# Gate and u of an FFN tile by seven products of half-size blocks in place of eight, in a two-layer hybrid inference step

## The chip, the core and the metric

The kernel runs on one core of a Trainium2 chip. The metric is the time of one execution in device microseconds. An execution is one inference step of the whole network, and each time given below is the median of several executions or that of the one execution that the profiler recorded.

## What is computed

The network has two layers of width 1024 and works on 640 tokens, 128 of context and 512 latent ones. Layer 0 mixes tokens with a gated delta rule, layer 1 with a long convolution ("hyena"). Behind each mixer stand an out-projection and a feed-forward block (FFN), and this is the part that the change touches. Cut from the reference:

```python
def _rms_norm(x, g):
    xf = x.astype(jnp.float32)
    y = xf * lax.rsqrt(jnp.mean(xf * xf, axis=-1, keepdims=True) + EPS)
    return (y * g.astype(jnp.float32)).astype(x.dtype)

def _swiglu(h, w_gu, w_down):
    gu = h @ w_gu
    return (jax.nn.silu(gu[..., :D_FF]) * gu[..., D_FF:]) @ w_down
...
        ctx = ctx + mc[2] * oc
        lat = lat + ml[2] * ol
        ctx = ctx + mc[5] * _swiglu(_modulate(_rms_norm(ctx, norm2_g[layer]), mc[3], mc[4]),
                                    ffn_w_gu[layer], ffn_w_down[layer])
        lat = lat + ml[5] * _swiglu(_modulate(_rms_norm(lat, norm2_g[layer]), ml[3], ml[4]),
                                    ffn_w_gu[layer], ffn_w_down[layer])
```

`w_gu` is 1024 x 5632: its first 2816 columns make the gate, the other 2816 make u. `_modulate(h, shift, scale)` is `h * (1 + scale) + shift` with other vectors for context and latent tokens.

## The kernel before

Activations lie transposed: features on the 128 partitions, tokens along the free axis, so that a tensor of width 1024 is eight tiles of 128 x 640. TensorE (PE) multiplies in a reduced-precision 32-bit type, fp32r. So each operand is held as a high part, its cast to that type, and a low part, the rest; and one product is three matmuls, high x high, high x low and low x high, added in one PSUM bank. ScalarE (ACT) makes high parts by a cast, VectorE (DVE) makes low parts by a subtraction: for weights that is `wsplit`, lines 118 (`wh`) and 119 (`wl`), behind the load of a tile `raw` on SyncE's (SP) queue in `wload`. There are two buffers each of `wh` and `wl` and five of `raw`.

`out_gemm` makes the out-projection: eight rows `d`, each two halves of 24 matmuls into `ps_o`, which line 352 takes out of PSUM into the residual `x`. From each row `sumsq` (lines 247 and 248) adds up squares for the norm in `acc`, and `fold` (lines 303 to 308) makes the FFN's input as high and low parts `fh` and `fl` of 642 columns: two columns that carry the shift of context and latent tokens, then 640 tokens with the scale multiplied in. The factor of the norm itself is applied behind the products.

`ffn` walks over 22 column tiles `f` of 128 gate and 128 u columns, in three groups of 8, 8 and 6 tiles. A tile has two halves of the tokens, 322 and 320 columns wide, and in each half the gate product `ps_g` and the u product `ps_u`: 4 x 24 = 96 matmuls. Then VectorE multiplies both with the norm's factor `rbc` (lines 401 and 402), ScalarE takes Silu (line 404), VectorE multiplies gate and u (line 405), and lines 407 and 408 split the result into `hh` and `hl`. The shift arrives through the first two columns of the products, which lines 397 and 398 copy into `fb`. Behind a group stand eight down rows, `ps_d`, of 2 x 24 matmuls (2 x 18 in the third group), which line 416 adds to `x`. In the first tile the norm's factor is made: `rstd_columns` sums `acc` over partitions in `ps_ss`, `rsqrt` (lines 168 to 175) takes the inverse root on VectorE in small steps, and `rstd_rows` builds `diag` (line 270), spreads it by PE into `ps_rb` (line 276) and copies that to `rbc` (line 277).

During the third group the function `done(d)` is called behind each down row: in layer 0 it stores the row and makes the fold for the hyena mixer, in layer 1 it scales the row with the last norm's weight and transposes it for the output.

PSUM has a pool `pg` of three banks (tag "g") and in these regions a pool `pu` of five (tag "u"). A list scheduler of the framework sets the order on each engine from the written order and the dependencies, ahead of the run; an engine then runs its list in order. Each tag of a pool is a ring of buffers, and who takes a buffer waits until its last readers are done.

Of the kernel before, what the change touches and what calls it, by code (L numbers as in the profile page):

```python
# [25 lines left out]
KD = D // 128  # L26
# [4 lines left out]
RAWS = 5  # L31

# [55 lines left out]
class _Kernel:  # L88
# [153 lines left out]
    def sumsq(self, pool, acc, x, first):  # L242
        if first:
            self.A.activation(acc, x, AF.Square)
        else:
            sq = pool.tile([128, NTOK], F32, tag="sq", name="sq", bufs=1)
            self.A.activation(sq, x, AF.Square)
            self.V.tensor_add(acc, acc, sq)
# [62 lines left out]

    def split_x(self, k, src):
# [16 lines left out]
    def out_gemm(self, pool, pu, src, xs, gate, x_old, ab, bias=None):  # L329

        V = self.V
        fx = []
        acc = pool.tile([128, NTOK], F32, tag="acc", name="acc", bufs=1)
        x = []
        for d in range(KD):
            xo = pool.tile([128, NTOK], F32, tag="xo", name="xo", bufs=2)
            self.nc.sync.dma_start(xo, x_old[d])
            w = self.wtile(src, 0, KD, d * 128)
            xt = pool.tile([128, NTOK], F32, tag=f"x{d}", name=f"x{d}", bufs=1)
            for hf in range(2):  # L340
                psp, tag = (self.pg, "g") if (2 * d + hf) % 8 < 3 else (pu, "u")
                ps = psp.tile([128, 512], F32, tag=tag, name="ps_o")
                self.gemm(ps[:, :320], w, xs, HALVES[hf])
                for c, sl, pl in PIECES[hf]:
                    g = gate[:, c, d : d + 1]
                    if bias is not None:
                        ob = pool.tile([128, 320], F32, tag="ob", name="ob", bufs=2)
                        self.A.activation(ob[:, pl], ps[:, pl], AF.Identity, bias=bias[:, d : d + 1])
                        src_ = ob[:, pl]
                    else:  # L350
                        src_ = ps[:, pl]
                    V.scalar_tensor_tensor(out=xt[:, sl], in0=src_, scalar=g, in1=xo[:, sl],
                                           op0=ALU.mult, op1=ALU.add)
# [7 lines left out]
    def ffn(self, pool, pg, pu, layer, x, acc, xs, done):  # L361
# [3 lines left out]
        gate = self.mod[layer][:, :, 40:48]  # L365

        for f0, nf, slots in ((0, 8, range(8)), (8, 8, (8, 9, 10, 11, 0, 1, 2, 3)),
                              (16, 6, (12, 13, 8, 9, 10, 11))):
            hs = []
            for f in range(f0, f0 + nf):  # L370
                wg = self.wtile(I["ffn_w_gu"][layer], 0, KD, f * 128)
                wu = self.wtile(I["ffn_w_gu"][layer], 0, KD, DFF + f * 128)
# [6 lines left out]
                prods = []
                for hf in range(2):  # L380
                    fs = (slice(0, 322), slice(322, 642))[hf]
                    o = 2 - 2 * hf
                    p1 = pg.tile([128, 512], F32, tag="g", name="ps_g")
                    self.gemm(p1[:, : 320 + o], wg, xs, fs)
                    p2 = pu.tile([128, 512], F32, tag="u", name="ps_u")
                    self.gemm(p2[:, : 320 + o], wu, xs, fs)
                    prods.append((p1, p2))
                    if hf == 0 and rb is None:
                        rs = self.rstd_columns(pool, pu, "u", acc)
# [1299 lines left out]
```

## Time and profile before

| | |
|---|---|
| median of three runs | 2105.75 us (2103.25 to 2108.15) |
| the profiled execution, its own time | 2103.4 us |
| span of that execution in the trace | 2101.6 us |
| granted clock of TensorE, mean over the span | 0.989 |
| matmuls in the trace | 13779 |
| DMA | 237.01 MB, 113 GB/s in the mean |

A page of the profile lists the busy time of each engine, its share of the span, the chain of work that ended last, and groups of instructions by line, with busy time, mean duration of one in ns, idle time in front of them and who ended it. PEld is the loading of weights into TensorE, which runs beside the matmuls. The trace is the same execution instruction by instruction, with start times in us from the start of the span.

### The profile page before, as it was taken

The numbers are of one execution on the slowest core, as the hardware profiler recorded it, in microseconds if no ns is written. First come the engines' busy times: TensorE is split into PE (matmuls) and PEld (weight loads), VectorE is DVE, ScalarE is ACT, GpSimd is POOL, SyncE is SP. The second block draws the span as 40 slices with busy tenths as digits, with TensorE's granted clock in tenths as the row PEclk, the third lists the DMA queues.
The fourth block names the chain that finished last, engine by engine and source line by source line (L and its number), as shares of the span: only waits on it lengthen the run. The fifth ranks groups of instructions, "written<-read, shape, count | busy, mean of one in ns | idle before, by whom it ended". The sixth has DMA issues, their size and how long they took to land.

```text
span 2101.6 us, 34710 instructions
## 1 busy us (share of the span) xinstructions
PE 2033.6 (97%) x13779; PEld 1889.1 (90%) x13779; DVE 1260.7 (60%) x2649; ACT 794.1 (38%) x1761; POOL 135.6 (6%) x241
## 2 busy tenths in 40 slices
PE   7998999999989999999999999999999999999997
PEld 4677888988866899999999999999889999999997
DVE  6887887876654464434434467878775443443444
ACT  4456445555533443212222243333344321221222
POOL 0131011110110100000000001010000000000000
PEclk8999999999989999999999999999999999999998
DMA  7856453344555632222222253222453222222221
GB/s 236 274 184 154 113 153 100 83 124 115 183 180 181 200 119 62 79 81 70 72 81 71 58 162 100 82 85 76 141 161 95 72 81 71 71 81 71 71 63 58
DMA packets 344833, 237.01 MB, mean 113 GB/s; under 512 B 62274, under 2 KB 314810, under 8 KB 344671
## 3 DMA queue, kind: packets, MB, share of 16 engines
q1 hardware_dynamic: 322495, 230.18, 36.7%
q10 hardware_dynamic: 22176, 4.62, 1.1%
q8 instruction: 108, 1.77, 0.4%
q14 instruction: 54, 0.44, 0.1%
HBM read 202.57 MB, written 32.19 MB: 112 GB/s over the span
## 4 chain that ended last, share of the span: by engine, by line
PE 81%; DVE 7%; ACT 4%; DMA 3%; issue 2%; POOL 0%; ACTq 0%; POOLq 0%; DVEq 0%
PE ps_g L131 15%; PE ps_u L131 15%; PE ps_d L131 15%; PE ps_hp L143 8%; PE ps_o L131 5%; PE ps_p L143 4%; PE ps_ada L209 2%; PE ps_ab L1467 2%; PE ps_g L1524 2%; PE ps_gate L143 1%; PE ps_s L1248 1%; PE ps_s L1214 1%; PE ps_y L1161 1%; PE ps_s L1225 1%; DMA ft<-fa 1%
## 5 line engine op out<-in xcount | busy, mean ns | idle before, releaser
L118 ACT CAST wh<-raw 128x1024 fp32r<-128x1024 f32 (+2 forms) x241 | 220.8, 921 | 461.3 <-PE ps_d L131 199.3
L119 DVE TENSOR_TENSOR wl<-raw,wh 128x1024 fp32r<-128x1024 f32 (+2 forms) x241 | 257.2, 1071 | 79.1 <-ACT wh L118 78.1
L131 PE MATMUL ps_g<-fh,wh 128*128 128x320 f32 (+1 forms) x704 | 220.2, 313 | 0.0
L131 PE MATMUL ps_g<-fh,wl 128*128 128x320 f32 (+1 forms) x704 | 219.6, 312 | 0.0
L131 PE MATMUL ps_u<-fh,wh 128*128 128x320 f32 (+1 forms) x704 | 219.5, 312 | 0.0
L131 PE MATMUL ps_u<-fh,wl 128*128 128x320 f32 (+1 forms) x704 | 219.4, 312 | 0.0
L131 PE MATMUL ps_g<-fl,wh 128*128 128x320 f32 (+1 forms) x704 | 218.0, 310 | 0.0
L131 PE MATMUL ps_u<-fl,wh 128*128 128x320 f32 (+1 forms) x704 | 217.9, 310 | 0.0
L416 DVE SCALAR_TENSOR_TENSOR x<-ps_d,mod,x 128x128 f32<-128x128 f32 x144 | 58.8, 437 | 154.0 <-PE ps_d L131 153.9
L131 PEld LDWEIGHTS ps_g<-fl,wh 128*128 128x128 f32 x704 | 133.6, 190 | 0.4 <-DVE fl L308 0.2
L131 PEld LDWEIGHTS ps_g<-fh,wh 128*128 128x128 f32 x704 | 133.5, 190 | 0.3 <-ACT fh L307 0.2
L131 PEld LDWEIGHTS ps_u<-fh,wh 128*128 128x128 f32 x704 | 133.6, 190 | 0.0
L131 PEld LDWEIGHTS ps_u<-fl,wh 128*128 128x128 f32 x704 | 133.4, 190 | 0.0
L131 PEld LDWEIGHTS ps_u<-fh,wl 128*128 128x128 f32 x704 | 132.8, 189 | 0.0
L131 PEld LDWEIGHTS ps_g<-fh,wl 128*128 128x128 f32 x704 | 132.5, 188 | 0.0
L143 PE MATMUL ps_p<-xh,wh 128*128 128x320 f32 x384 | 128.4, 334 | 1.8 <-ACT junk L1000 0.9
L143 PE MATMUL ps_hp<-xh,wh 128*128 128x322 f32 (+1 forms) x384 | 123.0, 321 | 0.7 <-DVE xp L1415 0.7
L143 PE MATMUL ps_p<-xh,wl 128*128 128x320 f32 x384 | 122.5, 319 | 0.0
L143 PE MATMUL ps_p<-xl,wh 128*128 128x320 f32 x384 | 122.2, 318 | 0.0
L143 PE MATMUL ps_hp<-xh,wl 128*128 128x320 f32 (+1 forms) x384 | 119.5, 311 | 0.0
L143 PE MATMUL ps_hp<-xl,wh 128*128 128x320 f32 (+1 forms) x384 | 119.4, 311 | 0.0
L131 PE MATMUL ps_d<-xh,wl 128*128 128x320 f32 x384 | 118.8, 309 | 0.0
(376 smaller groups left out, 5110.7 us busy)
## 6 DMA issues: line engine op xcount, KB each, us to landing
raw<-in_ada_w_dram SPq DMA_DIRECT2D x96, 512.0 KB
raw<-in_ffn_w_gu_dram SPq DMA_DIRECT2D x88, 512.0 KB
raw<-in_gdn_w_in_dram SPq DMA_DIRECT2D x33, 512.0 KB
raw<-in_ffn_w_down_dram SPq DMA_DIRECT2D x32, 512.0 KB
raw<-in_hy_w_in_dram SPq DMA_DIRECT2D x24, 512.0 KB
h_lat<-hlo SPq DMA_DIRECT2D x16, 512.0 KB
hs<-h_lat SPq DMA_DIRECT2D x32, 256.0 KB
raw<-in_ffn_w_down_dram SPq DMA_DIRECT2D x16, 384.0 KB
```

The lines of the kernel that those rows point to most:

```text
L118: self.A.copy(wh[:, ks, :], v[:, ks])
L119: self.V.tensor_sub(wl[:, ks, :], v[:, ks], wh[:, ks, :])
L131: self.PE.matmul(ps, a[:, k, :], b[:, sl], start=(n == 0), stop=(n == 3 * nk - 1))
L143: self.PE.matmul(ps, a[:, k, :], b[:, sl], start=(n == 0), stop=(n == 3 * nk - 1))
L209: PE.matmul(ps[32 * j : 32 * j + 32, :], self.sc[:, k, :], loaded[j * 512 // n][:, c : c + 512], start=(k == 0), stop=(k == KD - 1), skip_ ...
L416: V.scalar_tensor_tensor(out=x[d][:, sl], in0=p1[:, pl], scalar=gate[:, c, d : d + 1], in1=x[d][:, sl], op0=ALU.mult, op1=ALU.add)
L1161: PE.matmul(ps[:, n : n + 128], tm[:, d, t, :], cur[:, d, t, :], start=True, stop=True)
L1214: PE.matmul(pss[d][:, 0:128], qk[:, t, c * 128 : c * 128 + 128], state[seq, d], start=True, stop=True)
L1225: PE.matmul(p2, lt[:, d, t, c, :], ys[d], start=True, stop=True)
L1248: PE.matmul(pss[d][:, 256:384], ktok[:, t, c, :], ws[d], start=True, stop=True)
L1467: PE.matmul(ps, a_[:, m, it, js], b_[it], start=(c == 0), stop=(c == 5))
L1524: PE.matmul(pv[:, gi * 256 : gi * 256 + 256], a_[:, e, cs], b_[:, m, jt, :], start=(c == 0), stop=(c == 11))
```

## The change

The gate and u products of a tile are one product of blocks: the weights are split into two halves along the 1024 input features and into gate and u, the activations into the same two halves of features and into two halves of the tokens (322 columns each, both now with the two shift columns). Two by two blocks by two by two blocks take eight block products of 4 feature tiles x 3 matmuls; Winograd's form of Strassen's scheme takes seven, of sums of blocks, 84 matmuls in all.

- `quarters` replaces `fold` in `out_gemm`: from rows `k` and `k + 4` it makes the seven sums of activation blocks and splits each into a high part `qh` and a low part `ql`, 322 wide. The rows come in the order 0, 4, 1, 5, 2, 6, 3, 7.
- `gu_weights` makes the weights of a tile, one tile ahead of its products: it splits g in two halves, makes four sums `ws` of blocks on VectorE and splits those and one block of u into `ph` and `pl` (five buffers each).
- `gu_products` runs the seven products. Product 0's bank is copied by ScalarE into the bank in which product 2 goes on; that bank is copied after product 2 into the bank in which product 5 goes on; products 3, 4 and 6 go on in the bank of product 0 and twice in that of product 2. The matmuls that go on have no start flag.
- In `ffn` ScalarE copies product 1 to `t`, and VectorE adds `t` to two of the banks. The u results carry the opposite sign, which a negated gate of the down rows takes back. Four matmuls `ps_0` at the start of the FFN write the banks that are continued.
- The weights of the next group's first tile are made at down row 6 of a group, in front of row 7's own weights. In layer 0 `done(d)` for d of 3 and more is called behind the last down row, and the third group's `hh`, `hl` lie in other buffers.

The core of the diff:

```diff
+    def quarters(self, pool, k, hf, x, a, b, part, q):
+        A, V = self.A, self.V
+        kk = k + 4 * hf
+        f = pool.tile([128, 2, 322], F32, tag="s", name="fx", bufs=SUMS)
+        A.copy(f[:, :, 0:2], _bc(b[:, :, kk], 1, 2))
+        A.activation(f[:, 0, 2:130], x[:, 0:128], AF.Copy, scale=a[:, 0, kk : kk + 1])
+        A.activation(f[:, 0, 130:322], x[:, 128:320], AF.Copy, scale=a[:, 1, kk : kk + 1])
+        A.activation(f[:, 1, 2:322], x[:, 320:640], AF.Copy, scale=a[:, 1, kk : kk + 1])
+        B = part.setdefault(k, {})
+        B[2 * hf], B[2 * hf + 1] = f[:, 0], f[:, 1]
+        def out(i, src):
+            h, l = q[i, k] = [pool.tile([128, 322], F32R, tag=f"q{c}{i}{k}", name=f"q{c}") for c in "hl"]
+            A.copy(h, src)
+            V.tensor_sub(l, src, h)
+        tmp = lambda c: pool.tile([128, 512], F32, tag=c, name="ft", bufs=PARTS)[:, :322]
...
-        for d in range(KD):
-            xo = pool.tile([128, NTOK], F32, tag="xo", name="xo", bufs=2)
+        for n, d in enumerate((0, 4, 1, 5, 2, 6, 3, 7)):
...
-            fx.append(self.fold(*fs, d, xt, *ab))
+            self.quarters(pool, d % 4, d // 4, xt, *ab, part, fx)
...
+    def gu_weights(self, pool, layer, f, res):
+        A, V = self.A, self.V
+        W = self.I["ffn_w_gu"][layer]
+        g = self.wload(W, 0, KD, f * 128)
+        u = self.wload(W, 0, KD, DFF + f * 128)
+        def plus(x, y):
+            s = pool.tile([128, 2, 322], F32, tag="s", name="ws", bufs=SUMS)
+            s = s.rearrange("p a b -> p (a b)")[:, :512].rearrange("p (k f) -> p k f", k=4)
+            V.tensor_add(s, x, y)
+            return s
+        def out(i, src):
+            h, l = [pool.tile([128, 4, 128], F32R, tag=t, name=t, bufs=PARTS) for t in ("ph", "pl")]
+            A.copy(h, src)
+            V.tensor_sub(l, src, h)
+            res[i] = h, l
+        h, l = self.wsplit(g, 2)
+        res[0], res[3] = (h[:, 0:4], l[:, 0:4]), (h[:, 4:8], l[:, 4:8])
+        yield
+        s1 = plus(u[:, 0:4], u[:, 4:8])
+        out(1, s1)
+        yield
+        s2 = plus(s1, g[:, 0:4])
+        out(2, s2)
+        yield
+        yield
+        out(4, plus(g[:, 0:4], u[:, 0:4]))
+        yield
+        out(5, plus(s2, g[:, 4:8]))
+        yield
+        out(6, u[:, 4:8])
+        yield
+    def gu_products(self, pg, pu, f, w, q, banks):
+        A = self.A
+        def mul(i, ps, start):
+            wh, wl = w[i]
+            n = 0
+            for k in range(4):
+                xh, xl = q[i, k]
+                for a, b in ((wh, xh), (wh, xl), (wl, xh)):
+                    self.PE.matmul(ps[:, :322], a[:, k, :], b, start=start and n == 0, stop=n == 11,
+                                   skip_group_check=True)
+                    n += 1
+        b0 = banks[0] = pg.tile([128, 512], F32, tag="g", name="ps_g")
+        mul(0, b0, True)
+        b3 = banks[3] = pu.tile([128, 512], F32, tag=f"u{f % 2}", name="ps_u", bufs=1)
+        A.copy(b3[:, :322], b0[:, :322])
+        yield
+        b1 = banks[1] = pg.tile([128, 512], F32, tag="g", name="ps_gu")
+        mul(1, b1, True)
+        yield
+        mul(2, b3, False)
+        b2 = banks[2] = pu.tile([128, 512], F32, tag=f"u{2 + f % 2}", name="ps_g2", bufs=1)
+        A.copy(b2[:, :322], b3[:, :322])
+        yield
+        mul(3, b0, False)
+        yield
+        mul(4, b3, False)
+        yield
+        mul(5, b2, False)
+        yield
+        mul(6, b3, False)
+        yield
...
+        gate = pool.tile([128, 2, KD], F32, tag="ng", name="ng")
+        V.tensor_scalar(out=gate, in0=self.mod[layer][:, :, 40:48], scalar1=-1.0, scalar2=None, op0=ALU.mult)
+        zero = q[0, 0][0]
+        for n in range(4):
+            ps = pu.tile([128, 512], F32, tag=f"u{n}", name="ps_0", bufs=1)
+            self.PE.matmul(ps[:, :322], zero[:, :128], zero, start=True, stop=True)
+        last = range(5, -1, -1) if wide else (8, 3, 4, 5, 6, 7)
+        late = () if wide else range(3, KD)
...
+                prods = self.gu_products(pg, pu, f, cur, q, pb)
+                next(prods)
+                go(nxt)
+                next(prods)
+                t = pool.tile([128, 2, 322], F32, tag="g2", name="t", bufs=1)
+                A.copy(t[:, 0], pb[1][:, :322])
...
+                V.tensor_add(t[:, 1], pb[3][:, :322], t[:, 0])
+                go(nxt)
+                next(prods)
+                V.tensor_add(t[:, 0], pb[2][:, :322], t[:, 0])
...
                 wd = self.wtile(I["ffn_w_down"][layer], f0 * 128, nf, d * 128)
+                if d == KD - 2 and f0 < 16:
+                    nxt = self.gu_weights(pool, layer, f0 + nf, w)
+                    go(nxt, 7)
...
-                    done(d)
+                    if d not in late:
+                        done(d)
+        for d in late:
+            done(d)
```

In whole, PE has 528 matmuls of gate and u fewer and the eight of `ps_0` more in its order; VectorE has 2921 instructions in place of 2451, ScalarE's casts and copies rise likewise. Ahead of the first out-projection, and between the last fold of layer 0 and the second out-projection, the order of the engines is the same in both.

The order of VectorE in the middle of the first group of layer 0, before (lines of the code above; `xh_9204` and `xl_9205` are one tile's `hh` and `hl`):

```order
L401 TENSOR_TENSOR sg<-ps_g,rbc 128x320
L398 COPY fb<-ps_u 128x2
L402 TENSOR_TENSOR h<-ps_u,rbc 128x320
L405 SCALAR_TENSOR_TENSOR h<-h,fb,sg 128x128
L405 SCALAR_TENSOR_TENSOR h<-h,fb,sg 128x192
L408 TENSOR_TENSOR xl_9205<-h,xh_9204 128x320
L401 TENSOR_TENSOR sg<-ps_g,rbc 128x320
L119 TENSOR_TENSOR wl<-raw,wh 128x1024
L402 TENSOR_TENSOR h<-ps_u,rbc 128x320
L405 SCALAR_TENSOR_TENSOR h<-h,fb,sg 128x320
L119 TENSOR_TENSOR wl<-raw,wh 128x1024
```

And in a like place now: `ws` are sums of weight blocks, `ph` and `pl` their high and low parts, `t` is product 1 with what is added to it.

```order
L561 TENSOR_TENSOR xl4_9433<-h_9514,xh4_9432 128x320
L422 TENSOR_TENSOR pl_9631<-ws_9628,ph_9630 128x512
L416 TENSOR_TENSOR ws_9813<-ws_9781,raw_9756 128x512
L422 TENSOR_TENSOR pl_9663<-ws_9660,ph_9662 128x512
L416 TENSOR_TENSOR ws_9851<-raw_9756,raw_9758 128x512
L536 COPY fb_9587<-ps_g_9588 128x2
L537 TENSOR_TENSOR sg_9666<-ps_g_9588,rbc_8876 128x320
L122 TENSOR_TENSOR wl_9761<-raw_9756,wh_9760 128x512 x2
L541 TENSOR_TENSOR t_9626<-ps_u_9601,t_9626 128x322
L422 TENSOR_TENSOR pl_9701<-ws_9698,ph_9700 128x512
L548 TENSOR_TENSOR h_9667<-t_9626,rbc_8876 128x320
L416 TENSOR_TENSOR ws_9875<-ws_9813,raw_9756 128x512
```

Where two low parts `wl` stood between the steps of a tile, there are sums and low parts in halves of that width, set between the steps; a low part mostly belongs to a sum that was made about a tile earlier: `ws_9628`, `ws_9660` and `ws_9698` here are sums for the tile before the one of `ws_9813` and `ws_9851`. Of the 176 low parts of sums in the program 125 stand 19 to 33 rows behind their sum, and 8 within three rows.

VectorE in the first tile of layer 0, before, from the roots to the first multiplication (`rs` is the inverse root, one column for each 128 tokens):

```order
L174 SCALAR_TENSOR_TENSOR rs_t<-rs_t,ms 128x5
L175 SCALAR_TENSOR_TENSOR rs<-rs_t,rs 128x5
L173 TENSOR_TENSOR rs_t<-rs 128x5
L174 SCALAR_TENSOR_TENSOR rs_t<-rs_t,ms 128x5
L175 SCALAR_TENSOR_TENSOR rs<-rs_t,rs 128x5
L270 TENSOR_TENSOR diag<-ident,rs 128x640
L119 TENSOR_TENSOR wl<-raw,wh 128x1024 x2
L401 TENSOR_TENSOR sg<-ps_g,rbc 128x320
```

Now the steps of the root stand between weight sums:

```order
L422 TENSOR_TENSOR pl<-ws,ph 128x512
L177 SCALAR_TENSOR_TENSOR rs_t<-rs_t,ms 128x5
L416 TENSOR_TENSOR ws<-raw 128x512
L178 SCALAR_TENSOR_TENSOR rs<-rs_t,rs 128x5
L544 TENSOR_TENSOR t<-ps_g_8872,t 128x322
L176 TENSOR_TENSOR rs_t<-rs 128x5
L416 TENSOR_TENSOR ws<-ws,raw 128x512
L177 SCALAR_TENSOR_TENSOR rs_t<-rs_t,ms 128x5
L422 TENSOR_TENSOR pl<-ws,ph 128x512
L178 SCALAR_TENSOR_TENSOR rs<-rs_t,rs 128x5
L422 TENSOR_TENSOR pl<-ws,ph 128x512
L273 TENSOR_TENSOR diag<-ident,rs 128x640
```

`diag`, on which `ps_rb` waits, now has sums and low parts of the second tile's weights in front of it.

ScalarE at the end of the first group of layer 0, before (`wh_9970` to `wh_10147` are down rows 4 to 7, `wh_10206` and `wh_10212` g and u of tile 8):

```order
L118 CAST wh_9970<-raw_9968 128x1024
L118 CAST wh_10029<-raw_10027 128x1024
L118 CAST wh_10088<-raw_10086 128x1024
L118 CAST wh_10147<-raw_10145 128x1024
L118 CAST wh_10206<-raw_10204 128x1024
L303 CAST xh4_12852<-mod1_74 128x2
L303 CAST xh5_12911<-mod1_74 128x2
L303 CAST xh6_12970<-mod1_74 128x2
L118 CAST wh_10212<-raw_10210 128x1024
```

And now, where `wh_10362` is down row 6, `wh_10370` g of tile 8, `wh_10459` down row 7 and `wh_10538` g of tile 9:

```order
L121 CAST wh_10303<-raw_10301 128x1024
L121 CAST wh_10362<-raw_10360 128x1024
L121 CAST wh_10370<-raw_10366 128x512 x2
L121 CAST wh_10459<-raw_10457 128x1024
L121 CAST wh_10538<-raw_10534 128x512 x2
L463 COPY ps_u_10532<-ps_g_10519 128x322
L421 CAST ph_10561<-ws_10559 128x512
```

g of tile 8 has moved ahead of down row 7; of the two `wh` buffers, row 7 gets the one that row 6 used. On PE the row begins with two matmuls of each half (`ps_d_10463`, `ps_d_10490`), which need its high part alone, and five of tile 8's product 0, all ahead of the first that needs its low part `wl_10460`.

More of the change, by code (lines that the diff above doesn't have):

```diff
@@ L239, in norm_cols, with sumsq @@
         return a, b
-    def sumsq(self, pool, acc, x, first):
+    def sumsq(self, pool, acc, x, first, tag="g1"):
         if first:
@@ L363, in ffn, with go @@
+    def ffn(self, pool, pg, pu, layer, x, acc, q, done, wide):
         A, V, I = self.A, self.V, self.I
         rb = acc2 = None
-        gate = self.mod[layer][:, :, 40:48]
-        for f0, nf, slots in ((0, 8, range(8)), (8, 8, (8, 9, 10, 11, 0, 1, 2, 3)),
-                              (16, 6, (12, 13, 8, 9, 10, 11))):
+        gate = pool.tile([128, 2, KD], F32, tag="ng", name="ng")
[6 more added lines that the diff above has]
+        late = () if wide else range(3, KD)
+        w = {}
+        nxt = iter(())
+        def go(it, n=1):
+            for _ in range(n):
+                next(it, None)
+        for f0, nf, slots in ((0, 8, range(8)), (8, 8, range(8)), (16, 6, last)):
@@ L377, in ffn @@
                     hh, hl = [pool.tile([128, NTOK], F32R, tag=f"{c}{n}", name=c) for c in ("hh", "hl")]
+                hs.append((hh, hl))
                 bias = pool.tile([128, 2, 2], F32, tag="fb", name="fb", bufs=2)
[L379 to L389, printed above, removed]
@@ new lines, in ffn @@
+                if rb is None:
+                    rb = self.rstd_rows(pool, pg, "g", rs, "g1")
+                next(prods)
+                go(nxt)
+                sg = pool.tile([128, NTOK + 4], F32, tag="g1", name="sg", bufs=1)
+                h = pool.tile([128, NTOK], F32, tag="g0", name="h", bufs=1)
+                V.tensor_copy(bias[:, 0], pb[0][:, 0:2])
+                V.tensor_mul(sg[:, 0:320], pb[0][:, 2:322], rb[:, 0:320])
+                for c, sl, pl in PIECES[0]:
+                    A.activation(sg[:, sl], sg[:, sl], AF.Silu, bias=bias[:, 0, c : c + 1])
@@ new lines, in ffn @@
+                next(prods)
+                V.tensor_add(t[:, 1], pb[3][:, :322], t[:, 0])
+                go(nxt)
+                next(prods)
+                V.tensor_add(t[:, 0], pb[2][:, :322], t[:, 0])
+                go(nxt)
+                V.tensor_mul(sg[:, 320:640], t[:, 0, 2:], rb[:, 320:640])
+                A.activation(sg[:, 320:640], sg[:, 320:640], AF.Silu, bias=t[:, 0, 1:2])
+                V.tensor_mul(h[:, 320:640], t[:, 1, 2:], rb[:, 320:640])
+                V.scalar_tensor_tensor(out=h[:, 320:640], in0=h[:, 320:640], scalar=t[:, 1, 1:2],
+                                       in1=sg[:, 320:640], op0=ALU.add, op1=ALU.mult)
@@ new lines, in ffn @@
+                A.copy(hh[:, 320:640], h[:, 320:640])
+                V.tensor_sub(hl[:, 320:640], h[:, 320:640], hh[:, 320:640])
+                next(prods)
+                go(nxt)
+                V.tensor_copy(bias[:, 1], pb[3][:, 0:2])
+                V.tensor_mul(h[:, 0:320], pb[3][:, 2:322], rb[:, 0:320])
+                for c, sl, pl in PIECES[0]:
+                    V.scalar_tensor_tensor(out=h[:, sl], in0=h[:, sl], scalar=bias[:, 1, c : c + 1],
+                                           in1=sg[:, sl], op0=ALU.add, op1=ALU.mult)
@@ L1596, in run @@
                 nc.sync.dma_start(dst[:, 0:512], yt[t])
[L1597 removed]
+                y = self.xp.tile([128, NTOK + 2], F32, tag=f"x{'hl'[t % 2]}{6 + t // 2 % 2}" if t < 4
+                                 else "xh0", name="yb")[:, :512]
                 A.activation(y, last[t], AF.Copy, scale=rs[:, t : t + 1])
```

96 lines of the change are left out of this document (53 added, 43 removed).

## The prediction

> **What bounds the kernel now.** I read the page first: which engine is busy, and what the chain that ended last is made of.
>
> ```profile
> PE 2033.6 (97%) x13779; PEld 1889.1 (90%) x13779; DVE 1260.7 (60%) x2649; ACT 794.1 (38%) x1761; POOL 135.6 (6%) x241
> PE 81%; DVE 7%; ACT 4%; DMA 3%; issue 2%; POOL 0%; ACTq 0%; POOLq 0%; DVEq 0%
> ```
>
> PE is busy for 97% of the span and makes up 81% of the chain; VectorE (DVE) has 40% of the span free, ScalarE (ACT) 62%. Next, the chain in order of time, around the FFN of layer 0 (columns: start, length, engine, output, line, matmuls):
>
> ```profile
> 789.06 3.67 PE ps_g L131 x24
> 797.36 3.59 PE ps_g L131 x24
> 800.95 3.59 PE ps_u L131 x24
> 804.54 3.57 PE ps_g L131 x24
> 808.10 3.56 PE ps_u L131 x24
> ...
> 893.86 3.56 PE ps_u L131 x24
> 897.42 56.32 PE ps_d L131 x384
> 953.75 3.58 PE ps_g L131 x24
> ...
> 1064.54 3.56 PE ps_u L131 x24
> 1068.10 56.33 PE ps_d L131 x384
> ```
>
> From the second tile on, every product begins where the one before ended, and so do the down rows (`ps_d`): the FFN is one row of matmuls without a gap, and only their number and pace set its time. The products of 322 columns take 3.59, those of 320 take 3.57. What the others do meanwhile is in the windows, for the eight tiles of the second group (columns: length, then PE, weight loads, DVE, ACT and POOL busy, granted clock, DMA share, GB/s):
>
> ```profile
> 953.75:1068.10 114.35, 114.35 (x770) 114.35 (x770) 51.97 (x103) 33.44 (x57) 0.00 (x0) 1.00 0.24 70
> ```
>
> A tile is 114.35/8 = 14.29 us; VectorE works 6.5 of them, ScalarE 4.2, at full clock and a DMA share of 0.24. So PE sets the pace, and 7.8 us of VectorE are free in each tile.
>
> **Removed.** 84 matmuls a tile in place of 96, all 322 wide: 84 x 3.59/24 = 12.56 us. Over 44 tiles 44 x (14.29 - 12.56) = **-76.1 us**, if PE still never waits. All the rest is whether it does.
>
> **Added on VectorE and ScalarE, in every tile.** Rows by shape:
>
> ```profile
> L1479 DVE TENSOR_TENSOR t<-t,t 128x512 f32<-128x512 f32 x16 | 11.0, 685 | 0.1
> L401 DVE TENSOR_TENSOR sg<-ps_g,rbc 128x320 f32<-128x320 f32 x88 | 42.8, 487 | 50.7 <-PE ps_g L131 50.7
> L408 DVE TENSOR_TENSOR hl<-h,hh 128x320 fp32r<-128x320 f32 x40 | 19.6, 490 | 10.5 <-ACT hh L407 10.5
> L405 DVE SCALAR_TENSOR_TENSOR h<-h,fb,sg 128x320 f32<-128x320 f32 x44 | 24.2, 551 | 4.9 <-ACT wh L118 0.5
> L405 DVE SCALAR_TENSOR_TENSOR h<-h,fb,sg 128x192 f32<-128x192 f32 x44 | 18.1, 411 | 0.0
> L405 DVE SCALAR_TENSOR_TENSOR h<-h,fb,sg 128x128 f32<-128x128 f32 x44 | 15.4, 351 | 4.4
> L118 ACT CAST wh<-raw 128x512 fp32r<-128x512 f32 x64 | 38.6, 618 | 23.2 <-PE ps_p L143 21.6 <-DMA raw<-in_gdn_w_in_dram 0.8 <-ACT od L1233 0.4
> L407 ACT CAST hh<-h 128x320 fp32r<-128x320 f32 x40 | 18.4, 459 | 77.0 <-DVE h L405 77.0
> L404 ACT ACTIVATE sg<-sg,fb 128x320 f32<-128x320 f32 x44 | 24.6, 560 | 0.1
> L277 ACT COPY rbc<-ps_rb 128x320 f32<-128x320 f32 x8 | 3.2, 426 | 1.5 <-PE ps_rb L276 1.3
> ```
>
> VectorE now has 11 operations of 128x512 a tile (4 sums, 5 low parts of sums, 2 low parts of g): 11 x 0.685 = 7.54; four multiplications 4 x 0.487 = 1.95; two additions to `t`, 0.97; two low parts of h, 0.98; three scalar_tensor_tensors 0.551 + 0.411 + 0.351 = 1.31; two bias copies, about 0.3. That is 13.07 us in 24 instructions, *above* PE's 12.56. But the durations overlap, as a stretch without waits shows (start, length):
>
> ```profile
> 1465.91 0.69 DVE L1486 TENSOR_TENSOR yal<-t,yah 128x512 fp32r<-128x512 f32 x1
> 1466.52 0.69 DVE L1481 TENSOR_TENSOR t<-t,t 128x512 f32<-128x512 f32 x1
> 1467.12 0.69 DVE L1476 TENSOR_TENSOR t<-ps_ab,hs 128x512 f32<-128x512 f32 x1
> ```
>
> From start to start it is 0.61 and 0.60 for a duration of 0.69. With 0.085 less for each of 24 instructions VectorE needs 13.07 - 2.04 = 11.0 us, 1.5 below PE. I take that; the durations' own sum is the other bound. The Trainium skill, page "VectorE: DVE Perf Modes", section "The DRAIN you can't avoid", says that the next operation does not start until the pipe of the last is empty, though one that is not held starts earlier. By its first half the tile would be 13.07 and the sum 22 us higher; the 0.60 above speaks for the second half.
>
> ScalarE: 7 casts x 0.618, three PSUM copies x 0.43, Silu about 1.4, two casts of h x 0.459 = 7.9 us a tile, no bound.
>
> **Waits inside a tile.** Products, counted from 0, end every 1.79 us. ScalarE's copy of product 0 into the bank that product 2 continues may take from 1.79 to 3.58: a cast in front of it (0.62) and itself (0.43) leave 0.7. Its copy of that bank, after product 2, into the bank of product 5 must be over before product 4 adds to the copied bank, from 5.38 to 7.17: 5.38 + 0.62 + 0.43 = 6.4, slack 0.7 again. VectorE's addition of that bank into `t` after product 4 (8.96) must be over before product 6 begins at 10.75; behind one operation of 0.6 it ends near 9.6 to 10.1. All three hold, so I take 0 us. From product 6 to the next tile's product 3 (7.2 us) VectorE has some twelve operations, about 5.9 us, and two waits for casts of h, about 0.9: it fits by 0.4, and a delay there has 1.2 at product 6 before PE sees it. The upper bound is 0.5 us a tile (a second cast in front of a copy, 0.62 + 0.62 + 0.43 = 1.67, is still inside 1.79; a third, 2.29, is 0.5 over). The trace has no matmul that continues a sum written by ScalarE; the nearest row is the product itself at 3.59/24, which I take, and since it does the same reading and adding no gain is expected.
>
> **The first tile of a layer.** PE starts it at 780.56 and reaches the second tile at 797.36, 16.8 us, because `diag`, which feeds `ps_rb`, is late:
>
> ```profile
> 780.56 0.31 PE L131 MATMUL ps_g<-fh,wh 128*128 128x322 f32 x1
> 796.12 1.24 PE L276 MATMUL ps_rb<-diag,ones 128*128 128x320 f32 x4
> L248 DVE TENSOR_TENSOR acc<-acc,sq 128x640 f32<-128x640 f32 x35 | 28.7, 820 | 7.6 <-ACT sq L247 7.6
> L270 DVE TENSOR_TENSOR diag<-ident,rs 128x640 f32<-128x640 f32 x4 | 3.3, 823 | 0.1
> 780.76 0.55 DVE L352 SCALAR_TENSOR_TENSOR x<-ps_o,mod,xo 128x320 f32<-128x320 f32 x1 [2.34 <-PE ps_o L131]
> 789.50 0.17 DVE L173 TENSOR_TENSOR rs_t<-rs 128x5 f32<-128x5 f32 x1
> ```
>
> With 12 matmuls fewer it could be 15.0. But the order puts, between VectorE's last eviction of the out-projection and `diag`, 17 operations of 128x512 (weight sums of two tiles), nine of 128x322, `acc`, `diag` and a dozen small ones: 17 x 0.60 + 9 x 0.41 + 2 x 0.74 + 12 x 0.09 (0.17 less the overlap) + 0.75 for the eviction itself (0.55 and a handover of 0.2) = 17.2 us, then 1.24 for `ps_rb` and 0.43 for the copy to `rbc`: 18.9. I take +4 us a layer, **+8** (0 to +12; the four zero matmuls, 0.6 us, hide in it).
>
> **The end of groups one and two.** The weights of the next group's first tile now take one of the two `wh` buffers ahead of the last down row, so that row's split starts when row 6 has ended, not while it runs:
>
> ```profile
> L118 ACT CAST wh<-raw 128x1024 fp32r<-128x1024 f32 x161 | 168.9, 1050 | 401.1 <-PE ps_d L131 178.9 <-PE ps_g L131 82.4 <-issue 77.8
> L119 DVE TENSOR_TENSOR wl<-raw,wh 128x1024 fp32r<-128x1024 f32 x161 | 197.0, 1224 | 65.7 <-ACT wh L118 64.9
> ```
>
> PE waits for the cast, 1.05, with the handovers to ScalarE and back about 1.3 us; the subtraction behind it, 1.22, is covered by nine matmuls that the order sets there (9 x 0.149). Four times 1.35: **+5.4** (0 if the buffer came free earlier; 10 if the subtraction shows too).
>
> **Two ends.** A fold's main instructions on ScalarE and VectorE:
>
> ```profile
> 1253.86 0.71 ACT L307 ACTIVATE xh<-x,acol 128x512 fp32r<-128x512 f32 x1
> 1255.23 0.75 DVE L308 SCALAR_TENSOR_TENSOR xl<-x,acol,xh 128x512 fp32r<-128x512 f32 x1
> ```
>
> The last tile's h is ready later: bias copy, 0.487, 0.351, 0.411, the cast 0.459, 0.490 and handovers, about 2.8 us behind product 6. In groups of eight the seven older tiles cover 21 matmuls, 3.1 us; in the third group five cover 2.2: 0.5 a layer. At the entry of the hyena mixer five folds now wait for the last down row, each some 0.7 on both engines; PE has 33 matmuls, 4.9 us, to run ahead of the last: +0.5 (0 to 3). Together **+1.5**.
>
> The out-projection's seven quarters in place of two folds a row hide behind its eight rows of 48 matmuls (7.1 us each), but for the last, counted in the first tile. A tile still loads its two blocks of weights; in 12.56 us the DMA share goes from 0.24 to 0.27. Outside these two regions the order is unchanged.
>
> **Sum.** -76.1 + 8 + 5.4 + 1.5 = -61.2. The profiled run took 2103.4 us (span 2101.6): 2042.2. It lies 2.35 below the median of the three runs, 2105.75, so the forecast is 2044.5, given as **2044**.
>
> **Rivals.**
> *VectorE becomes the bound.* If its durations add up when each of a tile's 24 instructions has waits of its own, the tile is 13.07: 44 x 0.51 = +22 on the sum, **2067**. For it: only 1.5 us of slack by the overlapped times. The Trainium skill's rule named above, its first half, would make it so. Against: 0.60 for 0.69.
> *A copy between PSUM banks comes late* by up to 0.5 us a tile, since ScalarE takes its casts in a fixed order: +22, also **2066**.
> *Slower: VectorE idles through ScalarE's casts.* Each low part waits for a cast of a sum that VectorE itself made. The row of `wl<-raw,wh` shows 64.9/161 = 0.40 us of idle before one, and that of `hl<-h,hh` 10.5/40. Were nothing else ready in between, 5 x 0.618 + 2 x 0.459 = 4.0 us would come on top of 11.0: a tile of 15.0, 44 x 0.71 = +31 and the 14.9 of the other terms: **2152**. It turns slower than before where the tile passes 14.29 - 14.9/44 = 13.95, that is at 3.0 us of such idling. Against: in the order 125 of the 176 low parts of sums stand 19 to 33 rows, about a tile, behind their sum, so that the casts have long been made.
> *The waits just eat the gain*, a tile of 13.85 to 14.05: within 0.2% of **2105**. It needs the same idling at 2.8 to 3.1 us, a narrow strip.
> *PE does not get fewer matmuls* is excluded: the order has 528 fewer and 8 more.
>
> **How the numbers follow.** Forecast 0.66; VectorE bound 0.20; late copies 0.05; gain eaten 0.03; slower 0.06. Low end: only the removed matmuls, 2103.4 - 76.1 + 2.35 = 2029.6, so 2030. High end: VectorE bound at 2067 with another 0.25 us of waits a tile (11 us), 2078. The band of 0.2% (4.2 us, about what a measurement of this kernel can tell from no change) holds the eaten gain alone. Faster 0.91, same 0.03, slower 0.06.
>
> **What would show it.** Right: in the chain seven products of 12 matmuls at 1.79 or 1.80, tiles 12.6 apart; windows over a group with PE without gaps, VectorE near 11 to 13 busy a tile. First tile near 19 us; PE idle 1.3 before the last down row of groups one and two. Wrong: tiles over 13 us apart, with PE's idle time released by VectorE's `pl` (VectorE bound or idling: the idle column of the `pl` rows tells which) or by the copies of `ps_u` and `ps_g2`.

## The result and the profile after

The changed kernel takes 2044.61 us (median of four runs, 2042.82 to 2051.41), the kernel before 2106.26 us (2103.25 to 2108.15). The ratio is 0.9715 (95% interval 0.9688 to 0.9741), 61.7 us less. The forecast was 2044, with a range of 2030 to 2078.

The profiled execution took 2051.4 us, span 2049.6. The page's first and fourth part:

```profile
PE 1967.1 (96%) x13259; PEld 1818.0 (89%) x13259; DVE 1498.7 (73%) x3175; ACT 949.3 (46%) x2185; POOL 135.5 (7%) x241
PE 76%; DVE 10%; DMA 5%; ACT 4%; issue 2%; POOL 1%; ACTq 0%; POOLq 0%; DVEq 0%; SPq 0%
```

PE is busy for 66.5 us less with 520 matmuls fewer, VectorE for 238 us more with 526 instructions more (3175 for 2649 in the traces), and PE is still busy for 96% of the span. The chain around the FFN of layer 0 (start, length, engine, output, line, matmuls; the listing gives the longest pieces only, which leaves products out):

```profile
808.02 2.05 PE ps_g L456 x12
811.85 1.79 PE ps_u L456 x12
...
824.37 1.79 PE ps_u L456 x12
827.95 1.81 PE ps_u L456 x12
831.53 1.79 PE ps_u L456 x12
836.89 1.79 PE ps_u L456 x12
...
895.92 49.33 PE ps_d L134 x335
947.95 6.47 PE ps_d L134 x44
957.25 1.79 PE ps_u L456 x12
...
1053.84 49.49 PE ps_d L134 x335
1106.04 6.47 PE ps_d L134 x44
...
1186.89 42.58 PE ps_d L134 x288
1229.46 7.30 PE ps_hp L146 x48
```

From one product 2 to the next, 824.37 to 836.89, a tile is 12.52 us, where it was 14.29. The windows of the second group's eight tiles (length, then PE, weight loads, DVE, ACT, POOL, clock, DMA share, GB/s) and the waits of PE over the whole FFN of layer 0 (microseconds in all, times, longest) show what is left:

```profile
953.67:1053.84 100.17, 100.17 (x675) 100.17 (x674) 84.34 (x173) 55.00 (x113) 0.00 (x0) 1.00 0.29 85
```

```profile
PE ps_d L134 <- ACT wh L121: 2.0, 2, 1.0
PE ps_rb L279 <- DVE diag L273: 1.8, 1, 1.8
PE ps_g L456 <- ACT ps_u L463: 1.2, 1, 1.2
PE ps_u L456 <- ACT ps_g L470: 0.5, 1, 0.5
```

In the tiles PE has no gap, VectorE is at 84%, ScalarE at 55%. The five waits are all at the edges: two at the last down row of a group, three in the first tile. In layer 0 the first tile runs from here to the 808.02 above (the four matmuls are `ps_0`):

```profile
788.33 0.77 PE L491 MATMUL ps<-qh 128*128 128x322 f32 x4
806.68 1.34 PE L279 MATMUL ps_rb<-diag,ones 128*128 128x320 f32 x4 [1.76 <-DVE diag L273]
```

Both executions by stage (from the chain and the timelines; the forecast is the sum of the prediction's terms in that stage; layer 0 and layer 1 stand side by side where a cell has two values):

| stage, us | before | after | difference | forecast |
|---|---|---|---|---|
| start to the first FFN matmul of layer 0 | 780.56 | 788.33 | +7.8 | 0 |
| first tile, layers 0 and 1 | 16.80, 16.83 | 19.69, 19.80 | +5.9 | +4.5 |
| tiles 1 to 7, layers 0 and 1 | 100.06, 100.07 | 87.90, 87.83 | -24.4 | -24.2 |
| down rows of group 1 and tiles of group 2 | 170.68, 170.67 | 157.92, 157.92 | -25.5 | -25.0 |
| down rows of group 2 and tiles of group 3 | 142.04, 142.04 | 133.05, 132.89 | -18.1 | -18.1 |
| last down rows of layer 0 | 42.24 | 42.57 | +0.3 | +0.5 |
| hyena and second out-projection | 359.00 | 360.98 | +2.0 | +0.5 |
| last down rows of layer 1 to the end | 60.61 | 60.72 | +0.1 | +0.5 |
| from the first FFN matmul to the end | 1321.04 | 1261.27 | -59.8 | -61.2 |

The first line lies where both kernels have the same order of instructions; the experiments return to it.

### The profile page after: what moved, and what is told of

It reads as the page before. It is cut to its first block, busy times and chain, and to the rows that moved or that the text cites. A ratio compares the mean times of both kernels' runs of the same rounds, so it can differ in the third digit from the quotient of the medians.

```text
span 2049.6 us, 34532 instructions
## 1 busy us (share of the span) xinstructions
PE 1967.1 (96%) x13259; PEld 1818.0 (89%) x13259; DVE 1498.7 (73%) x3175; ACT 949.3 (46%) x2185; POOL 135.5 (7%) x241
## 4 chain that ended last, share of the span: by engine, by line
PE 76%; DVE 10%; DMA 5%; ACT 4%; issue 2%; POOL 1%; ACTq 0%; POOLq 0%; DVEq 0%; SPq 0%
PE ps_d L134 15%; PE ps_g L456 11%; PE ps_u L456 11%; PE ps_hp L146 8%; PE ps_o L134 5%; PE ps_gu L456 4%; PE ps_p L146 3%; PE ps_ab L1626 2%; PE ps_ada L212 2%; PE ps_g L1683 2%; DVE cacc L1127 1%; PE ps_gate L146 1%; DMA ln<-ft 1%; PE ps_s L1407 1%; PE ps_y L1320 1%
## 5 line engine op out<-in xcount | busy, mean ns | idle before, releaser
L121 ACT CAST wh<-raw 128x512 fp32r<-128x512 f32 (+2 forms) x241 | 179.0, 763 | 278.0 <-PE ps_d L134 168.3
L122 DVE TENSOR_TENSOR wl<-raw,wh 128x512 fp32r<-128x512 f32 (+2 forms) x241 | 206.8, 873 | 35.5 <-ACT wh L121 34.5
L134 PE MATMUL ps_d<-xh,wh 128*128 128x320 f32 x688 | 212.9, 310 | 3.9 <-ACT wh L121 3.9
L134 PE MATMUL ps_d<-xl,wh 128*128 128x320 f32 x688 | 212.9, 310 | 0.0
L456 PE MATMUL ps_u<-qh,ph 128*128 128x322 f32 x528 | 164.9, 312 | 1.4 <-ACT ps_g L470 1.4
L456 PE MATMUL ps_u<-ql,ph 128*128 128x322 f32 x528 | 165.5, 313 | 0.0
L456 PE MATMUL ps_u<-qh,pl 128*128 128x322 f32 x528 | 163.8, 310 | 0.0
L134 PEld LDWEIGHTS ps_d<-xh,wh 128*128 128x128 f32 x688 | 129.2, 188 | 5.5 <-ACT wh L121 5.0
L134 PEld LDWEIGHTS ps_d<-xl,wh 128*128 128x128 f32 x688 | 129.2, 188 | 0.8 <-DVE xl L561 0.7
L134 PEld LDWEIGHTS ps_d<-xh,wl 128*128 128x128 f32 x688 | 129.3, 188 | 0.0
```

The costliest lines, as they stand in the source:

```text
L121: self.A.copy(wh[:, ks, :], v[:, ks])
L122: self.V.tensor_sub(wl[:, ks, :], v[:, ks], wh[:, ks, :])
L134: self.PE.matmul(ps, a[:, k, :], b[:, sl], start=(n == 0), stop=(n == 3 * nk - 1))
L456: self.PE.matmul(ps[:, :322], a[:, k, :], b, start=start and n == 0, stop=n == 11, skip_group_check=True)
```

## The experiments

The theory was the prediction's: PE's matmuls alone set the tiles, and what is lost is lost at the last down row (two buffers of `wh`), and in the first tile (`diag` behind weight sums). The rivals were that VectorE has no room, that the copies between banks have none, and that a wait taken away only moves.

**again**: the changed kernel as it is.

> The changed kernel once more, as it is, beside the kernels below. Theory: the median lies within 2 us of 2044.6. In its stages: a tile every 12.52 us, the first tile of a layer 19.7, each end of groups one and two 1.4 above its matmuls. The profiled execution on record took 7.8 us longer than the one of before up to the out-projection of layer 0, where both have the same order; if that was an accident of that execution, it is not there in another one, and the span is near 2042. Rival: the new kernel slows that part down, and then it stays, with a span near 2049.

Median 2046.15 us, span of the profiled execution 2048.7. Its first FFN matmul comes at 787.54 us, so most of the +7.8 is there again, as the rival says; from there to the end it takes 1261.1, with first tiles of about 19.7 and 12.52 for a tile, as expected. But other kernels with that same first part reached the place at 778.4 (no_sums), 779.8 (row7_first), 781.1 (sub_1) and 788.5 us (sub_10). In a like stretch of 135 us, which ends near the start of layer 0's out-projection, the granted clock (the column behind POOL) and PE's matmul count were, in the changed kernel's execution and in row7_first's:

```profile
600.00:735.00 135.00, 123.98 (x760) 93.53 (x759) 63.14 (x179) 51.86 (x151) 15.34 (x28) 0.90 0.61 187
```

```profile
592.00:727.00 135.00, 126.57 (x802) 95.28 (x801) 66.00 (x185) 53.21 (x156) 14.86 (x28) 0.94 0.64 195
```

So that part varies by up to 10 us between executions of the same instructions. The clock can be one share of it: in the mean from the start to the first FFN matmul it is 0.97 in the changed kernel's two executions and 0.98 in the one of before and in row7_first. It isn't all, as sub_10 is as late at 0.98. Nor does it seem to be the kernel: the changed kernel's other six executions have spans of 2041.0 to 2045.7 us, and if they too took 1261.2 behind it, the place came at 779.8 to 784.5 in them (an estimate). What else makes the part vary stays open. Below, the edits are compared by the time from the first FFN matmul to the end, 1261.2 us here.

**row7_first**: the last down row's weights ahead of the next group's.

```diff
-                if d == KD - 2 and f0 < 16:
+                if d == KD - 1 and f0 < 16:
```

> The next group's first weights are made behind the last down row's weights and not ahead of them. Theory (the last down row waits, since its two high and low buffers come free only when row 6 has ended): the wait of 1.0 us for the cast goes at all four ends, 4 x 1.43 = 5.7 us less in all, near 2039. Rival (the wait moves to the next group's first tile, whose weights are now made later, while row 7 runs): product 0 or 1 of that tile starts late by 1 to 2 us, and the total stays within 2 us of the changed kernel's.

Median 2041.89 us. The down rows of a group are one piece again, and of PE's waits in layer 0's FFN those for `wh` are gone:

```profile
887.39 56.50 PE ps_d L134 x384
1044.05 56.50 PE ps_d L134 x384
```

```profile
PE ps_rb L279 <- DVE diag L273: 1.8, 1, 1.8
PE ps_g L456 <- ACT ps_u L463: 1.2, 1, 1.2
PE ps_u L456 <- ACT ps_g L470: 0.5, 1, 0.5
```

In the changed kernel's execution (first line) ScalarE begins the cast for the last down row when PE is done with row 6; in row7_first's (second line) it begins it a row earlier, while PE works on row 6:

```profile
945.27 1.04 ACT L121 CAST wh<-raw 128x1024 fp32r<-128x1024 f32 x1 [5.90 <-PE ps_d L134]
929.74 1.05 ACT L121 CAST wh<-raw 128x1024 fp32r<-128x1024 f32 x1 [5.99 <-PE ps_d L134]
```

The down rows' 56.50 us stand against 56.33 before the change. The four stages shrink from 157.92, 133.05, 157.92 and 132.89 to 156.66, 131.62, 156.61 and 131.59: 5.3 us, against 5.7 expected, and no wait appears in the next group's first tile. So the wait was for the buffer that row 6 held, as the theory says. From the first FFN matmul to the end it takes 1254.6, 6.7 less, of which the other 1.4 is at the hyena mixer and a matter of the clock (below).

**pool_root**: the steps of the inverse root on GpSimd, as two products and a scale-and-add each.

```diff
-            V.tensor_mul(t, out, out)
-            V.scalar_tensor_tensor(out=t, in0=t, scalar=-0.5, in1=x, op0=ALU.mult, op1=ALU.mult)
-            V.scalar_tensor_tensor(out=out, in0=t, scalar=1.5, in1=out, op0=ALU.add, op1=ALU.mult)
+                eng.tensor_mul(t, out, out)
+                eng.tensor_mul(t, t, x)
+                eng.tensor_scalar(out=t, in0=t, scalar1=-0.5, scalar2=1.5, op0=ALU.mult, op1=ALU.add)
+                eng.tensor_mul(out, out, t)
```

> In the first tile of each layer the steps of the inverse root run on GpSimd, so that weight sums on VectorE no longer stand between them; diag has 11 operations of 128x512 ahead of it instead of 17. Theory (the first tile is long since diag is queued behind weight sums): PE's wait for diag, 1.8 us in layer 0 and 1.0 in layer 1, goes, and the first tile comes to 17.9 and 18.8 us; 2 to 3 us less in all. Rival (VectorE has too much to do in the first tile in whatever order): the wait appears elsewhere in the first two tiles, for pl of tile 1 or for the banks that wait for rbc, and the total stays within 1 us. If a step on GpSimd takes over 0.5 us, PE waits for diag longer than now.

Median 2042.72 us, but 1261.03 from the first FFN matmul: no gain, though the hyena stage is 1.4 shorter by the clock (below). The first group of layer 0 falls from 107.6 to 106.8 us, that of layer 1 rises to 109.7. Of this rise the clock has a part: right behind PE's wait for `diag` it falls to half for 3.4 us, which can cost up to 1.7 (length, PE, weight loads, DVE, ACT, POOL, clock, DMA share, GB/s):

```profile
1594.89:1598.30 3.41, 3.41 (x10) 2.63 (x10) 3.02 (x7) 2.13 (x5) 0.00 (x0) 0.50 0.19 55
```

In the next run, **both**, which has the same edit, the clock is full there, and the two first groups take 106.8 and 108.0: 0.8 less and 0.4 more than without the edit. `diag` in layer 1, in again and here, and two of the steps on GpSimd:

```profile
1607.03 0.81 DVE L273 TENSOR_TENSOR diag<-ident,rs 128x640 f32<-128x640 f32 x1
```

```profile
1593.74 0.82 DVE L284 TENSOR_TENSOR diag<-ident,rs 128x640 f32<-128x640 f32 x1 [1.76 <-POOL rs L180]
```

```profile
1589.47 0.19 POOL L177 TENSOR_TENSOR rs_t<-rs 128x5 f32<-128x5 f32 x1
1590.91 0.52 POOL L177 TENSOR_TENSOR rs_t<-rs 128x5 f32<-128x5 f32 x1
```

`diag` starts 14.1 us after the layer's first FFN matmul (1579.61), where in again it was 17.5 (1589.55). But VectorE idles 1.76 for GpSimd's result, and the new order has `ps_rb` 27 matmuls earlier on PE (21 in layer 0), which waits 1.64 us for `diag` where it had waited 1.0. In layer 0 that wait falls from 1.8 to 1.1, so that the two together are as long as before. The rival holds: the wait moved and did not go.

**both**: row7_first and pool_root together.

> Both edits together, the weights of the last down row first and the inverse root on GpSimd. Theory: the gains add, 7.5 to 8.5 us below the changed kernel, near 2036. Rival: at least one of them only moves a wait, and it is 5.7 or less.

2039.56 us; 1254.7 from the first FFN matmul, within 0.1 of row7_first's own value. Only one of the two gains is there, as the rival has it.

**sub_1** and **sub_5**: low parts of weights made twice, in sub_1 that of product 6 (the edit shown), in sub_5 those of products 1, 2, 4, 5 and 6.

```diff
             V.tensor_sub(l, src, h)
+            if i in (6,):
+                V.tensor_sub(l, src, h)
```

> One of the seven low parts of weights that VectorE makes in a tile is made twice (the low part of u's block), 0.6 us more of VectorE a tile. Theory (PE sets the pace and VectorE's 2.0 us of idle time in a tile can be filled): a tile stays at 12.52 us and the total within 2 us of the changed kernel's. Rival (VectorE's idle time in a tile is bound up in waits for casts, so that the tile has no room): 13.1 us a tile, 26 us more.

> All five low parts of sums are made twice, 3.0 us more of VectorE a tile, 10.5 + 3.0 = 13.5 us of work. Theory: VectorE becomes the bound, a tile takes 13.5 to 14.5 us, by how much of its waits for casts stays; 44 to 87 us more, so about the time of the kernel before or up to 2% above it at most. Rival (the busy times overlap still further, or waits are filled completely): under 13.0.

sub_1: 2042.7 us; the eight tiles of the second group, and VectorE in them:

```profile
947.03:1047.20 100.17, 100.17 (x675) 100.17 (x674) 88.03 (x180) 55.01 (x113) 0.00 (x0) 1.00 0.29 85
```

They take 100.17 us as without, with 3.7 us more of VectorE. The room is there, and the theory is right. But 173 instructions became 180, not 181: a group of eight makes the weights of seven tiles. In sub_5, at 2071.38 us in its one execution, that counts. The long pieces of its down rows start here:

```profile
901.56 48.28 PE ps_d L134 x329
...
1062.71 48.28 PE ps_d L134 x329
...
1196.17 40.68 PE ps_d L134 x277
```

From one group's rows to the next are 161.15 us in place of 157.92: 3.2 us for eight tiles, 0.4 a tile, where the theory had 1 or more. A tile there is 12.9 us, under the rival's 13.0. The theory's reckoning by single tiles was wrong: from the second group on, the first tile's weights are made in the down rows. Most of what sub_5 costs, 10.3 and 10.5 us, lies in the first groups of the two layers. By groups VectorE's work is 8 x 4.46 us (on products) + 7 x 6.65 (on weights), each sum from the durations less their overlap of 0.085: 82.2 us in the second group, against 84.34 measured and PE's 100.17.

**sub_10** tests that reckoning: the five low parts made three times.

> All five low parts of sums are made three times, 6.05 us more of VectorE for each tile's weights. sub_5 cost 3.2 us a group of eight tiles, not 8 or more: a group of eight makes the weights of only seven tiles, since those of its first are made in the down rows. Theory by groups: 8 x 4.46 us of work on products and 7 x (6.65 + 6.05) on weights are 124.6 us against PE's 100.2, so the second group with the down rows ahead of it, 157.9 us, grows by 24.4; the third, 6 x 4.46 + 5 x 12.7 = 90.3 against 75.1, by 15.2 from 132.9; over both layers some 128 us. Rival by tiles: VectorE 16.6 a tile against 12.5, 4.1 x 8 = 33 and 25, over both layers 180.

```profile
929.76 48.28 PE ps_d L134 x329
...
1110.48 48.56 PE ps_d L134 x329
...
1258.12 41.64 PE ps_d L134 x282
```

The second and third groups take 180.72 and 147.64 us: 22.8 and 14.7 more, with 24.4 and 15.2 expected by groups, 33 and 25 by tiles. In all it is 1400.8 us from the first FFN matmul in the one execution, 140 more, where 128 were expected. The difference is in the first groups, which take 33.6 and 34.6 more and not 24.4. Layer 0's, in the changed kernel and in sub_10:

```profile
788.33:895.92 107.59, 104.15 (x694) 102.71 (x693) 95.53 (x205) 61.29 (x126) 0.00 (x0) 1.00 0.30 89
788.53:929.76 141.23, 117.67 (x700) 107.32 (x699) 140.22 (x284) 61.24 (x126) 0.00 (x0) 0.96 0.20 59
```

There VectorE has the first tile's work too, and 79 low parts more where seven tiles have 70; it is busy for 140.2 of 141.2 us. So VectorE's limit is a group's. The changed kernel stands 15.8 us under it in the second group and 12.1 in the first.

**copy_5**: each copy between banks made five times.

```diff
-        A.copy(b3[:, :322], b0[:, :322])
+        for _ in range(5):
+            A.copy(b3[:, :322], b0[:, :322])
```

(and the same for the copy from `b3` to `b2`)

> Each of the two copies between PSUM banks is made five times in a row, 4 x 0.36 = 1.4 us longer. By the trace the copies end 1.05 and 0.94 us before the product that waits for them. Theory (that is all the room): products 2 and 4 start 0.4 and 0.5 us late, a tile is 13.4 to 13.7 us, 40 to 52 us more. Rival (the scheduler finds other matmuls to set in front, or ScalarE's casts give way): under 10 us more. If it is far more, the later casts of ScalarE are late too, and ScalarE is nearer to its bound than its 55% say.

2061.89 us in its one execution; 1276.5 from the first FFN matmul, 15.3 more. Of these, 10.1 come up to the end of the first groups' down rows in the two layers together, and only 1.9 in a later group of eight. In both first tiles the clock was at 0.50 for 6.8 us, which can make up to 6.8 of the 10.1. The scheduler had set products and casts in another order, with product 0 of the next tile and in some tiles a part of its product 1 ahead of a tile's products 4 to 6. The rival is nearer; what the copies cost in the unchanged order was not measured, and that there is 0.9 us of room rests on the trace alone.

**no_sums**: the weight sums left out.

```diff
-        s1 = plus(u[:, 0:4], u[:, 4:8])
-        out(1, s1)
+        out(1, u[:, 0:4])
...
+        res[2] = res[4] = res[5] = res[1]
```

> The kernel leaves out the four sums of weight blocks and takes plain blocks of u for all of them; one high and low part serves four products. VectorE has seven operations of 128x512 fewer a tile, ScalarE three or four casts fewer. Theory (in the tiles only PE's matmuls count): a tile stays at 12.52 us; in the first tile diag has fewer operations in front, and the wait of 1.8 and 1.0 us for it goes, so that the total is 2 to 5 us lower. Rival (the sums' traffic or waits still slow PE): a tile is under 12.45 us, 3 us or more on top of that.

2043.01 us; 1259.4 from the first FFN matmul, 1.8 less. The stages of groups two and three are 158.09, 132.88, 157.92 and 132.89: as with the sums, to 0.2 us. So neither sums nor their traffic slow PE. The wait for `diag` is gone in both first tiles; layer 0's first group takes 105.4 us, but layer 1's 109.4. There PE now waits 2.6 us for a cast `ph` of product 1 that stands behind the out-projection's casts on ScalarE, and the clock is at 0.50 for the next 6.8 us, which can cost up to 3.4.

**root_2**: row7_first, and two steps of refinement of the root in place of three.

```diff
-        for _ in range(3):
+        for _ in range(steps):
...
-                    rs = self.rstd_columns(pool, pg, "g", acc)
+                    rs = self.rstd_columns(pool, pg, "g", acc, 2)
```

> The last down row's weights first, as in row7_first, and the inverse root of the first tile with two steps of refinement on VectorE in place of three, which takes three small operations, and the weight sums between them, from in front of diag; PE's order keeps ps_rb at its place in layer 0 and has it 5 matmuls earlier in layer 1. The output differs by the third step, some parts in a million. Theory (diag is late because each step of the root queues behind a sum or low part of 0.6 us): diag comes some 1.8 us earlier, the first group of layer 0 falls from 107.6 to 105.8 or 106, that of layer 1 from 107.6 to 106.6 or 107; with the last rows' gain near 1252 us from the start of the first FFN to the end, 2.5 below row7_first. Rival (as with GpSimd, the wait only moves): each stays within 0.5 of 107.6.

2034.23 us, ratio 0.967 (0.9652 to 0.9688) to the kernel before; 1251.6 from the first FFN matmul, 1252 expected. The first groups take 105.56 and 106.16, and PE's waits in layer 0 have no `diag` left:

```profile
PE ps_g L456 <- ACT ps_u L463: 1.2, 1, 1.2
PE ps_u L456 <- ACT ps_g L470: 0.5, 1, 0.5
```

`diag` starts 15.4 us after the first FFN matmul of layer 0 in place of 17.5. Three operations of 0.16 us are not 2.1 us; so `diag` was late by the root's chain, each step of which stands behind another operation, most of them of 0.6 us (rows in the next section). With its slightly rougher root this is the fastest of the kernels; of those that compute what the change computes, row7_first and both share the first place.

## Why the prediction came out right

- **Removed**, -76.1: right. The tile is 12.52, not 12.56, since a product takes 1.79 from its start to the next one's; 44 x 1.77 = 77.9.
- **Waits inside a tile**, 0: right. PE has no gap in any tile behind a layer's first one, and no_sums and sub_1 give the same 12.52 with less and more VectorE work. That durations overlap was right too: 4.46 + 6.65 = 11.1 us of VectorE belong to a tile, near the 11.0 worked out, and the 84.34 in the windows are less than eight times that because only seven tiles' weights fall into them. The reckoning by tile was the weak point: the room is a group's, 15.8 us in the second group, where the prediction had 1.5 x 8 = 12. The rival in which VectorE becomes the bound was weaker than it looked by tiles: the durations of the group's 173 operations, end to end and without any overlap, add up to 94.3 us, still under PE's 100.17. The Trainium skill's rule that an operation waits for the emptied pipe (page "VectorE: DVE Perf Modes", section "The DRAIN you can't avoid"), which the same section takes back for an operation that is not held, was reckoned in the prediction at 13.07 us a tile, 104.6 for eight. By the group it comes to those 94.3 us and would not have slowed the tiles; and the trace has VectorE busy for 84.34, with the overlapped starts (0.60 for 0.69) again.
- **First tile**, +4 each over 15.0: 19.69 and 19.80 are +4.7 and +4.8. The cause was as forecast, the queue on VectorE ahead of `diag`. VectorE between the last eviction and `diag`, and what follows a step of the root:

```profile
788.53 0.55 DVE L396 SCALAR_TENSOR_TENSOR x<-ps_o,mod,xo 128x320 f32<-128x320 f32 x1 [1.20 <-PE ps_o L134]
...
803.68 0.16 DVE L176 TENSOR_TENSOR rs_t<-rs 128x5 f32<-128x5 f32 x1
803.75 0.68 DVE L416 TENSOR_TENSOR ws<-ws,raw 128x512 f32<-128x512 f32 x1
804.36 0.16 DVE L177 SCALAR_TENSOR_TENSOR rs_t<-rs_t,ms 128x5 f32<-128x5 f32 x1
...
805.81 0.82 DVE L273 TENSOR_TENSOR diag<-ident,rs 128x640 f32<-128x640 f32 x1
```

  `diag` ends at 806.63, 18.3 us after PE's last row of the out-projection; 17.2 were forecast. The missing 1.1 is a wait of 0.76 for a cast and small gaps. Not foreseen: the copies from bank to bank are late there by 1.2 and 0.5 us, since ScalarE still has the out-projection's casts. They cost nothing while `diag` is later still, and are what remains in root_2.

  The prediction misread the first tile of the kernel before, though: it put its 16.8 us down to a late `diag`. `diag` stood here, and was done 4.0 us ahead of `ps_rb` (796.12):

```profile
791.30 0.83 DVE L270 TENSOR_TENSOR diag<-ident,rs 128x640 f32<-128x640 f32 x1
```

  PE has no wait in those 16.8 us; they are its matmuls, those of the norm among them. The sum did not suffer, since it only took twelve matmuls off the 16.8.
- **End of groups one and two**, 1.35 each: right, with 1.43 (from 895.92 to product 2 at 957.25 are 61.33, against 56.32 + 3.58). row7_first takes back 1.3 of it.
- **Two ends**, +1.5: 0.3 and 0.1 for the two third groups, less than the 0.5 each. At the hyena mixer +2.0 in the profiled execution, but 359.5 to 359.6 us, +0.5 as forecast, in row7_first, pool_root, both, sub_1, sub_10, copy_5, no_sums and root_2. The other 1.5, which again and sub_5 have as well, is a lowered clock (below).

The sum was 1.4 us off between the first FFN matmul and the end, and in the median 0.6 us; that the median fits still better than the terms is luck, as the part before varies by 10 us.

## What to carry to other kernels

Where PE runs without a gap, a scheme with fewer matmuls is worth its matmuls times their pace, if the other engines' added work fits into a stage of PE's work, counted over the group in which it may be shifted and by start-to-start times rather than durations. The price is at the edges: count how many buffers a prefetch takes from the last consumer ahead of it, and what newly stands between the small steps of a serial chain. A chain moved to an idle engine gained nothing here, as the scheduler moved its consumer forward as well. And where one execution's clock can fall for a few microseconds, look at the granted clock of a stage before an edit is given the credit or the blame for 1 or 2 us there.

## What was not expected of the hardware

In the changed kernel's execution 12 matmuls at the entry of the hyena mixer ran at about half pace, 0.27 us from start to start in place of 0.149, behind short gaps:

```profile
1242.55 1.34 PE L279 MATMUL ps_rb<-diag,ones 128*128 128x320 f32 x4 [1.10 <-DVE diag L273]
1244.59 0.61 PE L146 MATMUL ps_hp<-xh,wh 128*128 128x320 f32 x1 [0.70 <-DVE xp L1574]
1245.00 0.47 PE L146 MATMUL ps_hp<-xl,wh 128*128 128x320 f32 x1
1245.27 0.47 PE L146 MATMUL ps_hp<-xh,wl 128*128 128x320 f32 x1
```

```profile
1243.00:1251.00 8.00, 7.30 (x37) 6.74 (x36) 3.87 (x9) 3.69 (x7) 1.66 (x2) 0.79 0.19 57
```

The granted clock is 0.79 in those 8 us: 0.50 from 1244.53 to 1247.94 and 1.00 on both sides. In again and sub_5 there is a like stretch of 3.41 us at 0.50, in the other eight runs there is none, with the same two waits in all. In row7_first the same place, with the same two waits of 1.10 and 0.70 us, ran at 1.00:

```profile
1232.00:1240.00 8.00, 7.30 (x48) 6.81 (x47) 5.57 (x10) 4.21 (x7) 1.68 (x2) 1.00 0.31 86
```

The Trainium skill (page "TensorE: Matmul & The Clock Gate", section "Part 1: The HAM clock gate (the "warmup" mystery)") says that the clock is set by PE's activity in a window that runs freely, so that the same kernel fares differently from run to run. That the same place fares differently these two rows show; what sets the clock they do not.

GpSimd's operations on 128 x 5 took 0.19 us or 0.52 for the same instruction within one chain (in pool_root, above), and 0.27 or 0.60 us from start to start. Why is open.
